# A two-sided third unit in the first phase of a feed-forward layer

## The chip, the cores and the metric

The kernel runs on one core of a Trainium2 chip. The metric is the device time in microseconds (us) of one execution. TensorE (PE) multiplies, VectorE (DVE) and ScalarE (ACT) compute, SyncE (SP) issues the loads; each takes its instructions in the order in which they are written down for it, and they wait for each other through semaphores.

## The reference

The reference is an encoder of two layers on 256 tokens of width 2048, in float32. Each layer adds a mixer (attention and a gated recurrence in the first, pooling and grouped attention in the second) and a feed-forward part. Both layers' feed-forward is touched:

```python
def swiglu(x, w_gate, w_up, w_down):
    return (jax.nn.silu(x @ w_gate) * (x @ w_up)) @ w_down
...
        f = swiglu(x, ffn_w_gate[layer], ffn_w_up[layer], ffn_w_down[layer])
        x = layer_norm(DN_ALPHA * x + f, ln_ffn_g[layer], ln_ffn_b[layer])
```

The hidden width is 5632.

## The kernel before

**Precision.** Every operand is split into a rounded high part and a rest (xTh and xTl for x, yTh and yTl for the hidden columns, whi and wlo for weights). A product takes three matmuls of 128x512: high by low, high by high, low by high (`mm3`, L289 to L292).

**Weights.** A half is 512 KB of weights, two blocks of 128x512. `load_half` has SP load it into one of four buffers named raw (L168); ACT rounds it to whi (L127), DVE subtracts to get wlo (L128). The pairs whi and wlo have their own slots: four in the pool wp, and seven more from the pools that `open_ring` adds. While a half is on PE, a later one is loaded into a free slot, and ACT's whi waits for the slot. A half of a gate or up product lasts 12 matmuls on PE.

**Feed-forward.** The hidden width is cut into 11 units of 512 columns, in three phases (`PHASES`, L69): units 0 to 2, 3 to 6, 7 to 10. A phase computes its units and then multiplies by the matching rows of the down weights, four stretches of 512 output columns, which add up in res.

A unit of phase 0 is whole (`whole`, L507): all of the gate's halves add up in two PSUM banks acc, one for each of the two groups of 128 tokens, then all of up's in two banks mx. The gate passes through silu on ACT into sil, DVE multiplies it by up (L523), and some halves later PE transposes the product (`transpose4`, L274) into a bank that ACT and DVE read as yTh and yTl (L127, L128). The list `later` counts halves down (`half_done`) and then issues what is due; the transposes come 4 and 5 halves after the unit, for the third unit 2 and 3.

A unit of phases 1 and 2 is two-sided (`unit`, L455): gate and up of both groups of tokens go on at once in four banks, c11, c12, c21, c22. The 16 blocks of x are taken as 8 pairs. Five pairs take eight products, as in `whole`. The pairs of `SEVEN` (5, 6, 7) take seven, by a scheme that needs sums of blocks of x (the forms e, f, g, h; L409 to L431) and sums of blocks of weights (z, L445 to L447). Such a pair is loaded in one piece of 1 MB into the single buffer rs (L443); ACT casts it to sh (L444, and L127 for the sums), DVE computes z, sl (L448) and sl of the sums (L128). There is one buffer for rs and one for z, and two each for sh and sl. Four further banks take the products p1, p6, p5 and p7, which enter several of the sums and are added when the unit ends (L484 to L499).

**PSUM.** There are eight banks of 128x512. In phase 0 before the change they are acc (3), tr (2) and mx (3). With `open_banks("sides")` they become two sides, aside and bside, of four each: the four sums of a unit on one side, its p banks and transposes on the other, and the sides change places with each unit. A bank is given out again in turn, and its new user waits for the last reader of the old.

**Order.** The program is written in the order of the loops, and each instruction has a priority, raised by `tc.high_priority` (400 for loads and their casts, 1000 for gate products and some transposes' readers). A scheduler places each engine's instructions by these, and what it placed is the order on the engine.

Of the kernel before, what the change touches and what calls it, by code (L numbers as in the profile page):

```python
# [11 lines left out]
F32 = mybir.dt.float32  # L12
# [6 lines left out]
P = 128  # L19
# [4 lines left out]
NCH = 512  # L24
# [42 lines left out]
HELD = 6  # L67
FREE = 7
PHASES = ((0, 1, 2), (3, 4, 5, 6), (7, 8, 9, 10))  # L69


SEVEN = (5, 6, 7)
PAIRS_FIRST = (0, 1, 2, 3, 5, 4, 6, 7)
PAIRS = (0, 1, 5, 2, 3, 6, 4, 7)
PAIRS_LAST = (0, 1, 5, 2, 6, 3, 4, 7)
# [5 lines left out]
def trunk(ctx: ExitStack, tc: tile.TileContext, a, out):  # L81
# [9 lines left out]
    def open_banks(kind):  # L91

        if banks:
            banks["stack"].close()
        stack = ctx.enter_context(ExitStack())
        pool = stack.enter_context(tc.tile_pool(name="ps", bufs=1, space=PSUM, reuse_waits="tile"))
        banks.update(stack=stack, pool=pool, kind=kind, side=0)
# [22 lines left out]
    def mxp():  # L120
        return bank("mx", 3)
# [26 lines left out]
    first = [True]  # L148
# [33 lines left out]
    later = []  # L182
# [91 lines left out]
    def transpose4(src, hi, lo, ahead_by=0):  # L274
        t = trp()
        for k in range(4):
            transpose(t[:, k * P : (k + 1) * P], src[:, k * P : (k + 1) * P], ident)
        v = t.rearrange("p (k t) -> p k t", k=4)
        with tc.high_priority(offset=ahead_by):
            split(hi, lo, v)  # L280
# [174 lines left out]
    def unit(sp, pairs, sevens, w, lhs, forms, yT, opening):  # L455

        b = {n: side_bank() for n in ("c11", "c21", "c12", "c22")}
        begun = set()
        left = {n: 4 * (len(pairs) - len(sevens)) // 2 for n in b}
        for _, _, n in SEVEN_ORDER:  # L460
            left[n] = left.get(n, 0) + len(sevens)

        def product(name, x, wt):
            left[name] -= 1
            mm3(b[name], x, wt, name not in begun, left[name] == 0)
            begun.add(name)

        behind = [low[-n] if opening and n else None for n in BEHIND]
        for p in pairs:
            if p in sevens:  # L470
                if "p1" not in b:
                    b.update((n, side_bank(True)) for n in ("p1", "p6", "p5", "p7"))
                wt = load_seven(sp, w[p], behind.pop(0))
                for i, x, name in SEVEN_ORDER:
                    product(name, forms[p][x], wt(i))
            else:
                for n, ks in ((0, (2 * p, 2 * p + 1)), (1, (2 * p + 1, 2 * p))):
                    hi, lo = load_half(w[p][:, 2 * n : 2 * n + 2])
                    for tok in range(NT):
                        for kk in range(2):  # L480
                            product(f"c{tok + 1}{n + 1}", lhs(tok, ks[kk]), (hi[:, kk, :], lo[:, kk, :]))
                    half_done()
        with tc.high_priority(offset=1000):
            g0, w_, v, x = (sp.tile([P, NCH], F32, tag=n, name=n, bufs=1) for n in ("g0", "g1", "u0", "u1"))  # L484
            nc.scalar.copy(g0, b["p1"])  # L485
            nc.vector.tensor_tensor(w_, g0, b["p6"], op=sub)
            nc.vector.tensor_tensor(v, w_, b["p5"], op=add)
            nc.vector.tensor_tensor(w_, w_, b["p7"], op=add)
            nc.vector.tensor_tensor(x, w_, b["p5"], op=add)
            nc.vector.tensor_tensor(g0, g0, b["c11"], op=add)  # L490
            nc.scalar.activation(g0, g0, AF.Silu)
            nc.vector.tensor_tensor(v, b["c12"], v, op=sub)
            nc.vector.tensor_tensor(w_, w_, b["c21"], op=add)
            nc.scalar.activation(w_, w_, AF.Silu)
            nc.vector.tensor_tensor(x, b["c22"], x, op=sub)

            banks["side"] ^= 1
            for tok, (g, u) in enumerate(((g0, v), (w_, x))):
                nc.vector.tensor_tensor(g, g, u, op=mult)  # L499
                s = slice(tok * P, (tok + 1) * P)  # L500
                later.append([2 + tok, lambda g=g, s=s: transpose4(g, yT[0][:, :, s], yT[1][:, :, s], 1000)])

    def ffn(layer, xT, res, mix_pool, close_mix, keep, last):
        lhs = x_lhs(xT)
        w = a[f"gu{layer}"]

        def whole(c, pool, first):  # L507

            gouts = [acc() for _ in range(NT)]
            sil = {}  # L510

            def silu(tok):
                sil[tok] = pool.tile([P, NCH], F32, tag="sil", name="sil", bufs=3)
                nc.scalar.activation(sil[tok], gouts[tok], AF.Silu)

            mm_chunk([(w[c, i][:, :2], (2 * i, 2 * i + 1)) for i in range(8)], lhs, gouts, tok_major=first, after=silu)

            uouts = [mxp() for _ in range(NT)]
            y = new_yT()

            def gated(tok):
                with tc.high_priority(offset=1000):
                    nc.vector.tensor_tensor(sil[tok], sil[tok], uouts[tok], op=mult)  # L523
                s = slice(tok * P, (tok + 1) * P)
                later.append([(2 if c == PHASES[0][-1] else 4) + tok, lambda: transpose4(sil[tok], y[0][:, :, s], y[1][:, :, s])])

            mm_chunk([(w[c, i][:, 2:], (2 * i + 1, 2 * i)) for i in range(8)], lhs, uouts, after=gated)
            return y

        stack = ExitStack()  # L530
        forms, making = {}, []

        def make():
            with tc.issue_after(low[-1]):
                if next(making[0], "end") is None:
                    later.append([3, make])

        nxt = cdp = None
        groups = {}
        for pi, chunks in enumerate(PHASES):  # L540
            end = pi == len(PHASES) - 1
            for c in chunks:
                if pi == 0:
                    groups[c] = whole(c, mix_pool, c == 0)
                else:
                    groups[c] = new_yT()
                    pairs = PAIRS_FIRST if c == chunks[0] else PAIRS_LAST if c == chunks[-1] else PAIRS
                    sevens = SEVEN[:-1] if c == chunks[-1] else SEVEN
                    unit(sp, pairs, sevens, w[c], lhs, forms, groups[c], c == chunks[0])
            if pi == 0:  # L550
                close_mix()
                sp = later_pool(stack, f"sp{layer}")
                open_banks("sides")
                making.append(forms_of(sp, xT, forms))
                later.append([2, make])
            gl = [groups[c] for c in chunks]
            if end:
                stack.close()
                open_banks("uses")
                cdp = None if last else keep("cdc")  # L560
                open_ring(keep(f"er{layer}"), 4)
                open_ring(later_pool(stack, f"e{layer}"), 3)
                fp = later_pool(stack, f"g{layer}")
                nxt = None if last else new_xT()
            stats = new_stats()
            evac, norm = residual_tools(res, None, None, None, stats)
            for n in range(4):
                if cdp and n == 1:
                    consts.extend(cd_constants(cdp))
                if end and n == 1:  # L570
                    evac, norm = residual_tools(res, *load_gb(fp, layer, "ffn"), stats)
                outs = [acc() for _ in range(NT)]
                halves = [(a[f"down{layer}"][n, 2 * c + i], two(4 * ci + 2 * i)) for ci, c in enumerate(chunks) for i in range(2)]

                def after(tok):
                    with tc.high_priority(offset=1000 if end and n == 3 else 0):
                        evac(tok, n, outs[tok], pi == 0, end)
                        if end and n == 3:
                            norm(tok, nxt, out if last else None)

                mm_chunk(halves, y_lhs(gl), outs, tok_major=(end and n == 3), after=after)
            if not end:
                banks["side"] ^= 1
        if end:
            rings.pop()
            stack.close()
        return nxt
# [427 lines left out]
    xT = new_xT()  # L1015
# [11 lines left out]
    def later_pool(stack, name):  # L1027
        return stack.enter_context(tc.tile_pool(name=name, bufs=1, reuse_waits="tile"))
# [22 lines left out]
    xT = layer_end(0, a["ab_out"], AB_OUT_GROUPS, yT, False)  # L1051
# [119 lines left out]
```

## Time and profile before

| | us |
|---|---|
| median of 3 runs | 2190.62 (2190.13 to 2190.7) |
| profiled execution | 2193.0 |
| span of the profiled execution, first to last instruction | 2191.2 |
| PE busy | 2172.8 (99%) |
| DVE busy | 1557.9 (71%) |
| ACT busy | 1051.0 (48%) |

The profile is of one execution. The times of its rows count from the first instruction. A timeline row gives the start, the duration, the engine, the line and what is written from what; a bracket gives how long the engine stood idle before it and what ended that. An engine's next instruction can start some 0.08 us ahead of the end that is shown for the last, so what a sequence takes is read from the distance of the starts. A group row gives the number of instructions, their busy time in all and the mean of one in ns, and behind it the engine's idle time ahead of them.

Layer 0's phase 0 ends with the third unit, its up from 624.11 to 645.87 us, and down follows. Layer 1's feed-forward starts at about 1474 us.

### The profile page before, as it was taken

What the parts mean: (1) busy time and instruction counts of PE and PEld (TensorE: products, weight loads), DVE (VectorE), ACT (ScalarE), POOL (GpSimd) and SP (SyncE); (2) the same over time, 40 slices, a digit from 0 to 9 for tenths busy, and PEclk for the clock granted to TensorE, in tenths of its full rate; (3) what the DMA queues carried; (4) which work ended last, traced back from release to release, by engine and by line L of the source; (5) the groups of instructions that cost most, each with busy time, mean ns of one, the idle gap of its engine ahead of it and who ended that gap; (6) DMA issues with size and microseconds to landing.
All of it is one profiled execution on the core that took longest, in us unless ns stands there. A gap on an engine that the chain in (4) does not pass through costs nothing.

```text
span 2191.2 us, 26625 instructions
## 1 busy us (share of the span) xinstructions
PE 2172.8 (99%) x10048; PEld 1803.9 (82%) x10048; DVE 1557.9 (71%) x1954; ACT 1051.0 (48%) x1278; POOL 49.5 (2%) x51
## 2 busy tenths in 40 slices
PE   9999999999999999999999999999999999999997
PEld 7888888888888888888888888888888888888886
DVE  6886688677537788577786775676367896768865
ACT  6445544546425454444445554455344554445441
POOL 0000000000000000000000300000000000000000
PEclk9999999999999999999999999999999999999999
DMA  8555536684636555565548553647456555655473
GB/s 297 162 164 176 170 128 192 200 280 146 232 123 227 185 201 192 187 232 184 194 153 296 174 175 123 229 158 255 143 186 232 183 191 183 220 175 195 173 250 112
DMA packets 112850, 420.64 MB, mean 192 GB/s; under 512 B 13776, under 2 KB 16848, under 8 KB 105808
## 3 DMA queue, kind: packets, MB, share of 16 engines
q1 hardware_dynamic: 112720, 418.93, 57.0%
q8 instruction: 79, 1.29, 0.2%
q14 instruction: 51, 0.42, 0.1%
HBM read 416.78 MB, written 2.10 MB: 191 GB/s over the span
## 4 chain that ended last, share of the span: by engine, by line
PE 94%; DVE 3%; DMA 2%; issue 1%; SPq 0%; ACT 0%; DVEq 0%
PE acc L292 43%; PE bside L292 21%; PE aside L292 19%; PE mx L292 7%; DMA rs<-in_gu 2%; PE mx L729 1%; PE tr L124 1%; DVE wlo L128 1%; DVE sl L128 0%; DVE sl L448 0%; PE mx L775 0%; PE bside L124 0%; PE aside L124 0%; PE mx L988 0%; DMA raw<-in_ab_in 0%
## 5 line engine op out<-in xcount | busy, mean ns | idle before, releaser
L128 DVE TENSOR_TENSOR wlo<-raw,whi 128x1024 fp32r<-128x1024 f32 (+1 forms) x673 | 816.6, 1223 | 433.8 <-ACT whi L127 428.0
L127 ACT CAST whi<-raw 128x1024 fp32r<-128x1024 f32 (+1 forms) x673 | 703.5, 1051 | 815.0 <-PE acc L292 253.8
L292 PE MATMUL acc<-whi,xTl 128*128 128x512 f32 x864 | 343.2, 397 | 4.7 <-ACT whi L127 4.7
L292 PE MATMUL acc<-whi,xTh 128*128 128x512 f32 x864 | 339.8, 393 | 0.0
L292 PE MATMUL acc<-wlo,xTh 128*128 128x512 f32 x864 | 337.5, 393 | 0.1
L292 PE MATMUL acc<-whi,yTl 128*128 128x512 f32 x512 | 200.7, 392 | 0.1
L292 PE MATMUL acc<-whi,yTh 128*128 128x512 f32 x512 | 199.7, 390 | 0.0
L292 PE MATMUL acc<-wlo,yTh 128*128 128x512 f32 x512 | 197.6, 390 | 0.2 <-DVE wlo L128 0.2
L292 PEld LDWEIGHTS acc<-whi,xTl 128*128 128x128 f32 x864 | 162.9, 189 | 36.9 <-ACT whi L127 5.6
L292 PEld LDWEIGHTS acc<-wlo,xTh 128*128 128x128 f32 x864 | 162.7, 188 | 33.9 <-DVE wlo L128 1.1
L292 PEld LDWEIGHTS acc<-whi,xTh 128*128 128x128 f32 x864 | 163.1, 189 | 31.2
L292 PE MATMUL bside<-whi,xTl 128*128 128x512 f32 x336 | 131.9, 393 | 1.5 <-ACT g L485 1.1
L292 PE MATMUL aside<-whi,xTl 128*128 128x512 f32 x336 | 131.2, 391 | 0.2
L292 PE MATMUL bside<-whi,xTh 128*128 128x512 f32 x336 | 131.0, 390 | 0.0
L292 PE MATMUL aside<-whi,xTh 128*128 128x512 f32 x336 | 131.0, 390 | 0.0
L292 PE MATMUL bside<-wlo,xTh 128*128 128x512 f32 x336 | 128.2, 390 | 0.0
L292 PE MATMUL aside<-wlo,xTh 128*128 128x512 f32 x336 | 128.1, 390 | 0.0
L292 PEld LDWEIGHTS acc<-wlo,yTh 128*128 128x128 f32 x512 | 96.2, 188 | 20.6 <-DVE wlo L128 0.7
L292 PEld LDWEIGHTS acc<-whi,yTl 128*128 128x128 f32 x512 | 96.2, 188 | 19.8 <-DVE res L308 0.5
L292 PEld LDWEIGHTS acc<-whi,yTh 128*128 128x128 f32 x512 | 96.2, 188 | 19.3
L128 DVE TENSOR_TENSOR sl<-z,sh 128x2048 fp32r<-128x2048 f32 x44 | 100.7, 2288 | 6.4 <-ACT sh L127 5.7
L444 ACT CAST sh<-rs 128x1536 fp32r<-128x1536 f32 x44 | 65.2, 1482 | 74.6 <-DMA rs<-in_gu 33.7
(266 smaller groups left out, 3445.4 us busy)
## 6 DMA issues: line engine op xcount, KB each, us to landing
raw<-in_gu SPq DMA_DIRECT2D x264, 512.0 KB, 4.7
raw<-in_down SPq DMA_DIRECT2D x176, 512.0 KB, 4.0
raw<-in_ab_in SPq DMA_DIRECT2D x127, 512.0 KB, 4.0
rs<-in_gu SPq DMA_DIRECT2D x44, 1024.0 KB, 6.2
raw<-in_cd_in SPq DMA_DIRECT2D x40, 512.0 KB, 4.3
raw<-in_ab_out SPq DMA_DIRECT2D x32, 512.0 KB, 4.4
raw<-in_cd_out SPq DMA_DIRECT2D x32, 512.0 KB, 4.4
bias<-in_na_bias SPq DMA_DIRECT2D x32, 64.0 KB, 4.2
```

The costliest lines, as they stand in the source:

```text
L124: return nc.tensor.transpose(o, src, eye)
L127: nc.scalar.copy(hi, src)
L128: return nc.vector.tensor_tensor(lo, src, hi.bitcast(F32), op=sub).ins
L292: ins = nc.tensor.matmul(o, lhs[a], rhs[b], start=start and n == 0, stop=stop and n == 2)
L444: nc.scalar.copy(hi[:, :3], raw[:, :3])
L729: nc.tensor.matmul(m[:, 2 * h + s, :], kk[:, h, s * P : (s + 1) * P], qq[:, h, r * P : (r + 1) * P], start=True, stop=True,)
```

## The change

The third unit of phase 0 is computed as a two-sided unit, with `PAIRS` and the three pairs of `SEVEN`. What goes with it:

- The pool that held sil and seven of the slots for whi and wlo is closed, and the pool of the two-sided units (sp) opened, 6 halves into the second unit (`change_rooms`), no longer after the third. sil of the second unit is then in the buffers g0 and g1.
- The forms are made from there on, a step in each half (`make`, once every 3 halves before).
- The banks become sides between the second and the third unit.
- The second unit's transposes come 2 and 3 halves after it, into bside banks, and the two instructions that read each have priority 1000.
- The first unit of phase 1 still orders its pairs by `PAIRS_FIRST`, and its 1 MB loads wait as before.

```diff
@@ -504,13 +505,17 @@
-        def whole(c, pool, first):
+        def whole(c, first):
...
             def silu(tok):
-                sil[tok] = pool.tile([P, NCH], F32, tag="sil", name="sil", bufs=3)
+
+                if sps:
+                    sil[tok] = sps[0].tile([P, NCH], F32, tag=f"g{tok}", name=f"g{tok}", bufs=1)
+                else:
+                    sil[tok] = mix_pool.tile([P, NCH], F32, tag="sil", name="sil", bufs=3)
...
-                later.append([(2 if c == PHASES[0][-1] else 4) + tok, lambda: transpose4(sil[tok], y[0][:, :, s], y[1][:, :, s])])
+                later.append([(4 if first else 2) + tok, lambda: transpose4(sil[tok], y[0][:, :, s], y[1][:, :, s], 0 if first else 1000)])
...
-        forms, making = {}, []
+        forms, making, sps = {}, [], []
 
         def make():
             with tc.issue_after(low[-1]):
                 if next(making[0], "end") is None:
-                    later.append([3, make])
+                    later.append([1, make])
+
+        def change_rooms():
+            close_mix()
+            sps.append(later_pool(stack, f"sp{layer}"))
+            making.append(forms_of(sps[0], xT, forms))
+            later.append([1, make])
...
-                if pi == 0:
-                    groups[c] = whole(c, mix_pool, c == 0)
+                if c < 2:
+                    groups[c] = whole(c, c == 0)
+                    if c == 0:
+                        later.append([6, change_rooms])
+                    else:
+                        open_banks("sides")
                 else:
                     groups[c] = new_yT()
-                    pairs = PAIRS_FIRST if c == chunks[0] else PAIRS_LAST if c == chunks[-1] else PAIRS
-                    sevens = SEVEN[:-1] if c == chunks[-1] else SEVEN
-                    unit(sp, pairs, sevens, w[c], lhs, forms, groups[c], c == chunks[0])
-            if pi == 0:
-                close_mix()
-                sp = later_pool(stack, f"sp{layer}")
-                open_banks("sides")
-                making.append(forms_of(sp, xT, forms))
-                later.append([2, make])
+                    pairs, sevens = PAIRS, SEVEN
+                    if pi and c == chunks[0]:
+                        pairs = PAIRS_FIRST
+                    elif pi and c == chunks[-1]:
+                        pairs, sevens = PAIRS_LAST, SEVEN[:-1]
+                    unit(sps[0], pairs, sevens, w[c], lhs, forms, groups[c], pi and c == chunks[0])
```

DVE before, layer 0, from the products of the second unit (sil by mx) on; the wlo are those of the third unit's halves, tr the banks of the second unit's transposes. The numbers tell buffers apart.

```order
L523 TENSOR_TENSOR sil_5022<-sil_5022,mx_5026 128x512
L523 TENSOR_TENSOR sil_5024<-sil_5024,mx_5027 128x512
L128 TENSOR_TENSOR wlo_5382<-raw_5380,whi_5381 128x1024
L128 TENSOR_TENSOR wlo_5400<-raw_5398,whi_5399 128x1024
L128 TENSOR_TENSOR wlo_5418<-raw_5416,whi_5417 128x1024
L128 TENSOR_TENSOR wlo_5436<-raw_5434,whi_5435 128x1024
L128 TENSOR_TENSOR wlo_5454<-raw_5452,whi_5453 128x1024
L128 TENSOR_TENSOR yTl_5029<-tr_5250,yTh_5028 128x4x128
L128 TENSOR_TENSOR wlo_5472<-raw_5470,whi_5471 128x1024
L128 TENSOR_TENSOR yTl_5029<-tr_5275,yTh_5028 128x4x128
L128 TENSOR_TENSOR wlo_5505<-raw_5503,whi_5504 128x1024
```

Seven instructions after the first product DVE reads the first transposes, and none of them belongs to a 1 MB load.

DVE in the changed kernel, the same place; rs_5398 is the second 1 MB load of the third unit and rs_5467 the third, z and sl belong to them; the lines are one to five higher.

```order
L129 TENSOR_TENSOR wlo_5248<-raw_5246,whi_5247 128x1024
L528 TENSOR_TENSOR g0_5030<-g0_5030,mx_5034 128x512
L528 TENSOR_TENSOR g1_5032<-g1_5032,mx_5035 128x512
L448 TENSOR_TENSOR z_5401<-z_5401,rs_5398 128x512
L129 TENSOR_TENSOR wlo_5273<-raw_5271,whi_5272 128x1024
L129 TENSOR_TENSOR sl_5400<-z_5401,sh_5399 128x2048
L446 TENSOR_TENSOR z_5470<-rs_5467 128x1024
L129 TENSOR_TENSOR wlo_5328<-raw_5326,whi_5327 128x1024
L447 TENSOR_TENSOR z_5470<-z_5470,rs_5467 128x512
L448 TENSOR_TENSOR z_5470<-z_5470,rs_5467 128x512
L129 TENSOR_TENSOR wlo_5346<-raw_5344,whi_5345 128x1024
L129 TENSOR_TENSOR yTl_5037<-bside_5239,yTh_5036 128x4x128
```

The read of the first transposes (bside_5239) now follows the first z of the third load, and the last z of the second load, which sets rs free, stands ahead of both.

PE before, layer 0, at the second unit's first transposes, within the third unit's gate.

```order
L292 MATMUL acc_5177<-whi_5233,xTh1_3821 128x512
L292 MATMUL acc_5177<-wlo_5234,xTh1_3821 128x512
L124 MATMUL tr_5250<-ident_72,sil_5022 128x128 x4
L292 MATMUL acc_5176<-whi_5258,xTl0_3822 128x512
L292 MATMUL acc_5176<-whi_5258,xTh0_3820 128x512
L292 MATMUL acc_5176<-wlo_5259,xTh0_3820 128x512
```

PE goes on in acc, and the bank tr is used again only by the next transposes but one.

PE in the changed kernel, layer 0, at the first pair of seven products; bside_5289 is p1, bside_5290 p6, and bside_5291 is p5, whose bank is that of bside_5239. The transposes into bside_5239 and bside_5264 stand 24 and 12 matmuls ahead of the pair.

```order
L293 MATMUL aside_5202<-wlo_5273,xTh1_3821 128x512
L293 MATMUL bside_5289<-sh_5294,xTl0_3822 128x512
L293 MATMUL bside_5289<-sh_5294,xTh0_3820 128x512
L293 MATMUL bside_5289<-sl_5295,xTh0_3820 128x512
L293 MATMUL bside_5290<-sh_5294,fml_5116 128x512
L293 MATMUL bside_5290<-sh_5294,fmh_5115 128x512
L293 MATMUL bside_5290<-sl_5295,fmh_5115 128x512
L293 MATMUL aside_5199<-sh_5294,xTl0_3822 128x512
L293 MATMUL bside_5291<-sh_5294,fml_5116 128x512
L293 MATMUL bside_5291<-sh_5294,fmh_5115 128x512
L293 MATMUL bside_5291<-sl_5295,fmh_5115 128x512
L293 MATMUL aside_5199<-sh_5294,xTh0_3820 128x512
```

The third product of the pair writes a bank that the transposes had.

On SP the third unit's first 1 MB load stands between the raw loads of the second unit's last two halves, the second behind the raw load of its own second half, the third five raw loads later. In layer 1 the engines' orders are the same.

## Rows read from the trace of the kernel before

**Rows 1.** The page: span, busy time of the engines, and the chain of waits by engine.

```profile
span 2191.2 us, 26625 instructions
...
PE 2172.8 (99%) x10048; PEld 1803.9 (82%) x10048; DVE 1557.9 (71%) x1954; ACT 1051.0 (48%) x1278; POOL 49.5 (2%) x51
...
PE 94%; DVE 3%; DMA 2%; issue 1%; SPq 0%; ACT 0%; DVEq 0%
```

**Rows 2.** What PE waited for: engine, line, what was waited for, us in all, times, the longest.

```profile
PE acc L292 <- ACT whi L127: 4.7, 1, 4.7
PE bside L292 <- ACT g L485: 1.1, 2, 0.8
PE acc L292 <- DVE wlo L128: 0.2, 1, 0.2
```

**Rows 3.** PE's timeline: a block of transposes and the two matmuls behind it, then the first matmul of the third unit's up and the first of down.

```profile
567.79 0.60 PE L124 MATMUL tr<-ident,sil 128*128 128x128 f32 x4
568.14 0.47 PE L292 MATMUL acc<-whi,xTl 128*128 128x512 f32 x1
568.46 0.39 PE L292 MATMUL acc<-whi,xTh 128*128 128x512 f32 x1
...
624.11 0.39 PE L292 MATMUL mx<-whi,xTl 128*128 128x512 f32 x1
...
645.87 0.39 PE L292 MATMUL aside<-whi,yTl 128*128 128x512 f32 x1
```

**Rows 4.** Busy time by window: us, then for each engine busy us and instructions, the granted clock of PE as a share of full, the DMA share and GB/s. The first window holds the second and third unit, the second one down and the beginning of phase 1.

```profile
560.00:645.00 85.00, 85.00 (x385) 70.35 (x384) 35.54 (x34) 30.45 (x33) 0.00 (x0) 1.00 0.50 164
645.00:735.00 90.00, 90.00 (x402) 74.54 (x401) 66.19 (x66) 43.32 (x40) 0.00 (x0) 1.00 0.65 223
```

**Rows 5.** Groups of instructions by line and shape of DVE, and ACT's whi from the page: count, busy us, mean ns, idle time ahead.

```profile
L128 DVE TENSOR_TENSOR wlo<-raw,whi 128x1024 fp32r<-128x1024 f32 x671 | 815.2, 1224 | 432.8 <-ACT whi L127 426.9 <-PE acc L292 1.6 <-DMA raw<-in_ab_in 1.5
L128 DVE TENSOR_TENSOR sl<-z,sh 128x2048 fp32r<-128x2048 f32 x44 | 100.7, 2288 | 6.4 <-ACT sh L127 5.7
L448 DVE TENSOR_TENSOR sl<-rs,sh 128x1536 fp32r<-128x1536 f32 x44 | 77.1, 1753 | 26.6 <-ACT sh L444 26.6
L445 DVE TENSOR_TENSOR z<-rs 128x1024 f32<-128x1024 f32 x44 | 53.7, 1221 | 37.3 <-DMA rs<-in_gu 37.0
L446 DVE TENSOR_TENSOR z<-z,rs 128x512 f32<-128x512 f32 x44 | 30.1, 684 | 0.3
...
L128 DVE TENSOR_TENSOR yTl<-bside,yTh 128x512 fp32r<-128x512 f32 x16 | 10.9, 683 | 2.1 <-ACT yTh L127 2.1
...
L523 DVE TENSOR_TENSOR sil<-sil,mx 128x512 f32<-128x512 f32 x12 | 8.0, 682 | 0.2
```

```profile
L127 ACT CAST whi<-raw 128x1024 fp32r<-128x1024 f32 (+1 forms) x673 | 703.5, 1051 | 815.0 <-PE acc L292 253.8
```

**Rows 6.** Timelines of DVE, SP and ACT at the first 1 MB load of layer 0, in down of phase 0: the last two fs, the load's issue, its first use.

```profile
676.24 0.55 DVE L424 TENSOR_TENSOR fs<-xs 128x384 f32<-128x384 f32 x1
676.71 0.55 DVE L425 TENSOR_TENSOR fs<-xs,fs 128x384 f32<-128x384 f32 x1
```

```profile
677.35 0.33 SPq L443 DMA_DIRECT2D rs<-in_gu  x1
```

```profile
683.59 1.48 ACT L444 CAST sh<-rs 128x1536 fp32r<-128x1536 f32 x1 [0.32 <-DMA rs<-in_gu]
```

**Rows 7.** SP's and ACT's timelines at a 1 MB load of phase 1: a raw load, the 1 MB load, the next raw load, and the first use.

```profile
794.91 0.33 SPq L168 DMA_DIRECT2D raw<-in_gu  x1
797.83 0.33 SPq L443 DMA_DIRECT2D rs<-in_gu  x1
798.91 0.33 SPq L168 DMA_DIRECT2D raw<-in_gu  x1
```

```profile
802.68 1.48 ACT L444 CAST sh<-rs 128x1536 fp32r<-128x1536 f32 x1 [1.14 <-DMA rs<-in_gu]
```

**Rows 8.** The same of SP and DVE at two further 1 MB loads, and from the view of the buffer rs the time from issue to landing of all 44. A raw row with x2 or x4 stands for that many loads.

```profile
811.18 0.33 SPq L168 DMA_DIRECT2D raw<-in_gu  x1
812.98 0.33 SPq L443 DMA_DIRECT2D rs<-in_gu  x1
814.11 8.47 SPq L168 DMA_DIRECT2D raw<-in_gu  x4
...
2017.50 2.06 SPq L168 DMA_DIRECT2D raw<-in_gu  x2
2021.03 0.33 SPq L443 DMA_DIRECT2D rs<-in_gu  x1
```

```profile
819.87 1.23 DVE L445 TENSOR_TENSOR z<-rs 128x1024 f32<-128x1024 f32 x1
...
2028.49 1.23 DVE L445 TENSOR_TENSOR z<-rs 128x1024 f32<-128x1024 f32 x1 [0.67 <-DMA rs<-in_gu]
```

```profile
DMA to landing us min/median/max: 4.6/6.2/8.7
```

**Rows 9.** PE's and ACT's timelines at PE's longest wait after the start, where a unit follows a unit.

```profile
1097.30 0.39 PE L292 MATMUL aside<-sl,xTh 128*128 128x512 f32 x1
1098.50 0.50 PE L292 MATMUL bside<-whi,xTl 128*128 128x512 f32 x1 [0.82 <-ACT g L485]
1098.84 0.40 PE L292 MATMUL bside<-whi,xTh 128*128 128x512 f32 x1
```

```profile
1097.87 0.58 ACT L485 COPY g<-bside 128x512 f32<-128x512 f32 x1
```

**Rows 10.** PE's timeline at the start, and the core's span and mean granted clock.

```profile
4.73 0.80 PE L292 MATMUL acc<-whi,xTl 128*128 128x512 f32 x1 [4.73 <-ACT whi L127]
...
8.04 0.63 PE L292 MATMUL acc<-wlo,xTh 128*128 128x512 f32 x1
8.47 0.63 PE L292 MATMUL acc<-whi,xTl 128*128 128x512 f32 x1
8.90 0.44 PE L292 MATMUL acc<-whi,xTh 128*128 128x512 f32 x1
```

```profile
core 0: 2191.2 us, clock 0.998
```

## The prediction

> **What bounds the kernel now.** I read the page's busy line and chain of waits first, then the waits of PE, then PE's timeline, and last the lines of DVE and the timelines around the 1 MB loads. PE is busy 2172.8 of 2191.2 us, and 94% of the chain of waits is PE [rows 1]. After the start PE waits only 1.3 us by name: 1.1 us for the copy that opens a unit's end (ACT L485) and 0.2 us for one wlo [rows 2]. So a matmul less is a matmul's time less, and any wait that is put in front of PE is paid in full. In the third unit of layer 0 (gate from 601.5 us, up 624.11 to 645.87) 96 matmuls lie between the first rows of up and of down: (645.87 − 624.11) / 96 = 0.2267 us each. Four transposes in between cost PE about 0.35 + 0.32 − 0.2267 = 0.44 us [rows 3]. In that stretch PE is busy 85.00 of 85.00 us while DVE works 35.54 [rows 4]: DVE has room, but it takes its instructions in the order written.
>
> **What the change removes.** Three pairs of the third unit take seven products in place of eight, three matmuls each: 9 matmuls fewer a layer, 18 in all, 18 × 0.2267 = 4.08 us. Bytes loaded are the same, the raw loads only grow from 0.5 to 1 MB for those pairs.
>
> **What it moves at no cost.** The forms (xs, fs, fmh, fml) are made in the second unit's up instead of in down; the same instructions, on a DVE that has 49 of 85 us free there [rows 4]. The rings shrink from eleven whi and wlo to four, halfway through the second unit's gate. A half lasts PE 12 × 0.2267 = 2.72 us and DVE needs 1.14 us from start to start for its wlo; the later phases run on four already, and PE is busy 90.00 of 90 us there [rows 4]. If that cover were gone, each late half would show as a PE wait on wlo, of which there is 0.2 us now [rows 2]. The end of the third unit becomes that of a two-sided unit, ten DVE instructions in place of two, but down opens with the first unit's columns, and needs the third's four halves later.
>
> **What it adds: a wait behind a load.** The second unit's transposes go into two of the four bside banks. The first pair of seven products takes the other two for p1 and p6, and for p5 and p7 it must take the transposes' banks again, so PE stops before p5 until DVE has read the first of them (yTl). In before they had tr banks for which nobody waited. In the changed DVE queue that read stands behind the first z of the third 1 MB load, and DVE can't pass it. So the load's landing decides. The priority given to the reads does not lift yTl above that z.
>
> Set U = 0 at the third unit's first matmul. PE asks for the bank after 48 matmuls of two pairs, 7 of p1, p6 and c11, and two blocks of transposes: 55 × 0.2267 + 2 × 0.44 = 13.35.
>
> DVE's side, start to start as the timelines show it (0.08 under each duration): wlo 1.14, z 1.14 then 0.60 twice, sl 1.67 and 2.21, a gate's product 0.60, yTl 0.60 and 0.68 to its end [rows 5]; ACT's whi 1.05.
> - First load. Its buffer is that of xs, so it goes out after the last two fs. They stand behind the wlo whose whi slot comes free 108 matmuls before U: −24.5, whi to −23.45, wlo to −22.2, two fs of 0.47 to −21.2. The same sequence in before: fs at 676.24 and 676.71, issue 677.35, landed just before 683.59, 6.2 us [rows 6]. With 6.3 it is there at −14.9.
> - z 1.14, wlo 1.14, z 0.60, sl 1.67, z 0.68 free the buffer: the second load goes out at −9.6. The nearest row has a raw load 2.9 us ahead and another 1.1 behind: 797.83 to 802.68, 4.85 us at most [rows 7]. It lands at −4.8, while DVE still has wlo, wlo, sl 2.21 and wlo, 5.63 in all, until −4.0.
> - From −4.0: z 1.14, sl 1.67, wlo 1.14, z 0.60, wlo 1.14, two gate products 1.20, z 0.68: the third load goes out at +3.6.
> - The third load goes out 1.8 and 3.5 us behind two raw loads, and a third follows 1.1 later. Two loads in before stand exactly so: issued 812.98, used 819.87 (6.9 us); issued 2021.03, used 2028.49 with DVE waiting for it (7.5) [rows 8]. I take 7.2: +10.8. The group of all 44 gives 4.6 at least and 8.7 at most [rows 8].
> - Behind it z 1.14, wlo 1.14, z 0.60, z 0.60, wlo 1.14 and the read 0.68, with its release 5.4: +16.2.
> PE waits 16.2 − 13.35 = 2.85 us, and a restart costs 0.11 more (1098.50 to 1098.84 is 0.34 against 0.2267) [rows 9]: 2.96 a layer, 5.92 in two. The second read follows 1.7 us later, and PE needs its bank 2.5 us after the first, so p7 adds nothing.
>
> Before, no bank is awaited here, so the wait's price is bounded by the loads: third at 4.85 gives 13.85, a stall of 0.5 and with the restart 0.6; third at 8.7 gives 4.35; and if the second load took 7.4 too, 1.6 more, 5.95. The lower end is below that: with every load early DVE reads in time and the price is 0; a gain has no reason, since nothing here was awaited. I take 2.96, since two rows have the third load's very neighbours.
>
> On the load, the Trainium skill has another price (SBUF — State Buffer, "The DMA setup-cost knee"): about 2 us fixed and the bytes at 436 GB/s, an estimate of 4.4 us for 1 MB. By that the read would end near 13.4, and the sum would be the removed matmuls alone. The least of the 44 loads, 4.6, agrees with the skill's figure; the two beside raw loads, 6.9 and 7.5, do not, and this load has three beside it.
>
> Sum on the profiled execution: 2193.0 − 4.08 + 5.92 = 2194.8 us. It lies 2.4 us over the runs' median of 2190.62; the same difference, +1.84, on the median gives **2192.5 us**.
>
> **The rivals.** About 0.2% (4.4 us) is the least a measurement of this kernel can tell from no change: 2186.24 to 2195.0.
> - No stall worth naming, because the loads land alone (4.85 us) or DVE comes there early. For it: the least of the 44 loads is 4.6, one among traffic took 4.85, and DVE is idle for over half of this stretch. Against it: the two rows with these very neighbours. Time: 2190.62 − 4.08 + 2 × 0 to 0.6 = 2186.5 to 2187.7. Chance 0.15.
> - The slower side: the second load also meets traffic. Then third issue and read move by 1.6 us, and with 7.2 to 8.7 for the third the stall is 4.45 to 5.95, 5.3 with the restart on the mean, in each layer: 2190.62 − 4.08 + 10.6 = 2197.1. It decides from a stall of (4.38 + 4.08) / 2 = 4.2 us a layer. For it: the median of the 44 loads is 6.2, the most 8.7 [rows 8]. Against it: the one row with the second load's neighbours [rows 7]. Chance 0.15.
> - PE comes back from the stall at half pace. At the start ten matmuls from 4.73 to 8.90 stand some 0.43 us apart (8.04 to 8.47), the pace of the 1.2 GHz level, and from there at half of that; the run's mean granted clock is 0.998 [rows 10] and that of the stretch here 1.00 [rows 4]. 4.17 us so would cost 4.17 × (1 − 0.2267 / 0.427) = 1.95 a layer, 3.9 in all: 2196.4. Against it: the longest wait in before, 1.2 us, was followed by a spacing of 0.34 and no slow stretch [rows 9]; a wait of 3 us isn't in the trace. Chance 0.06. The Trainium skill tells of this rule (TensorE: Matmul & The Clock Gate, "HAM oscillation — how this bites in real kernels"): a PE that waits for data between groups falls back to the half clock. The wait of 1.2 us does not show it, and no row here has a longer one.
> - The end of the third unit holds down up: its p1 is copied by ACT behind a load's cast, as after 1097.30, where PE lost 1.20 − 0.23 + 0.11 = 1.1 us [rows 9]. Twice that on top of the forecast: 2194.7. Against it: p1 is complete 18 matmuls, 4.1 us, before down opens, and a cast and the copy take ACT 1.05 + 0.58. Chance 0.04.
>
> **How the numbers follow.** The forecast, a stall of 1 to 4.2 us a layer, has 0.60 and by itself 2188.5 to 2195.0. Faster: only the best of the first rival, 0.05. Same: the forecast, the rest of that rival and the last one, 0.74. Slower: the second and third, 0.21. The range goes from the first rival's time to the second's: 2186.4 to 2197.2.
>
> **What would show it.** In the profile after: PE's waits must list a bside matmul of L293 waiting for yTl (DVE L129), twice, 2 to 4 us each, at the first pair of seven products. DVE's waits must show z waiting for rs just before, and PE's matmul count must fall by 18. If PE's waits do not change, the first rival holds and the time falls by 4. A load that takes under 5 us or over 8 there, a slow spacing behind the wait, or PE waiting elsewhere (for whi, for g L486) would make the forecast wrong.

## The result and the profile after

| | us |
|---|---|
| changed kernel, median of 5 runs | 2199.43 (2197.53 to 2203.79) |
| kernel before, median of 5 runs | 2190.62 (2190.13 to 2191.64) |
| ratio, after to before | 1.0043, 95% interval 1.0032 to 1.0054 |
| forecast | 2192.5, range 2186.4 to 2197.2, no change that can be told |

The change makes the kernel slower: by 0.43% in the ratio, by 8.8 us between the medians. The time lies above the range. The page after, as [rows 1], and the core's clock, as [rows 10]:

```profile
span 2197.7 us, 26597 instructions
...
PE 2171.8 (99%) x10030; PEld 1802.9 (82%) x10030; DVE 1589.2 (72%) x1988; ACT 1059.2 (48%) x1280; POOL 49.9 (2%) x51
...
PE 92%; DVE 4%; DMA 2%; issue 1%; SPq 0%; ACT 0%; DVEq 0%
```

```profile
core 0: 2197.7 us, clock 0.996
```

PE issues 10030 matmuls where it issued 10048: the 18 are gone. Yet its busy time fell by 1.0 us and not by 4, which says that some of the others took longer. The clock, 0.998 before, says the same. What PE waited for, as [rows 2]:

```profile
PE bside L293 <- DVE yTl L129: 8.7, 2, 4.4
PE acc L293 <- ACT whi L128: 4.7, 1, 4.7
PE acc L293 <- DVE wlo L129: 0.2, 1, 0.2
```

The first row is new: a bside matmul waits for yTl, twice, 4.4 us at most. PE's timeline shows the place in layer 0 (p1, p6, one matmul of c11, then p5) and what follows:

```profile
601.50 0.39 PE L293 MATMUL aside<-whi,xTl 128*128 128x512 f32 x1
...
614.48 0.39 PE L293 MATMUL bside<-sl,fmh 128*128 128x512 f32 x1
614.71 0.39 PE L293 MATMUL aside<-sh,xTl 128*128 128x512 f32 x1
619.48 0.79 PE L293 MATMUL bside<-sh,fml 128*128 128x512 f32 x1 [4.39 <-DVE yTl L129]
620.08 0.63 PE L293 MATMUL bside<-sh,fmh 128*128 128x512 f32 x1
620.50 0.63 PE L293 MATMUL bside<-sl,fmh 128*128 128x512 f32 x1
...
623.49 0.60 PE L293 MATMUL aside<-sh,xTh 128*128 128x512 f32 x1
623.92 0.41 PE L293 MATMUL aside<-sl,xTh 128*128 128x512 f32 x1
624.16 0.39 PE L293 MATMUL bside<-sh,fml 128*128 128x512 f32 x1
```

Two losses stand here. From 614.71 to 619.48 are 4.77 us, 4.54 more than a matmul. From 619.48 to 623.92 ten matmuls begin in 4.44 us, 2.17 more than 10 × 0.2267: they stand 0.43 us apart, as at the start [rows 10]. The granted clock by window (the columns are those of [rows 4]) names the cause:

```profile
614.94:619.48 4.54, 0.15 (x1) 0.00 (x0) 4.50 (x7) 1.04 (x1) 0.00 (x0) 0.74 0.33 112
619.48:623.92 4.44, 4.44 (x11) 3.47 (x12) 2.81 (x3) 0.00 (x0) 0.00 (x0) 0.50 0.77 236
623.92:630.00 6.08, 6.08 (x28) 5.04 (x27) 3.61 (x2) 4.24 (x3) 0.00 (x0) 1.00 0.38 119
```

Over the wait the mean is 0.74, so the clock fell while PE stood still. Right behind the wait it is at 0.50, the 1.2 GHz level, and then at 1.00. The wait ends with DVE's read of the first transposes, and DVE's timeline tells what that stood behind:

```profile
607.96 2.29 DVE L129 TENSOR_TENSOR sl<-z,sh 128x2048 fp32r<-128x2048 f32 x1 [0.85 <-ACT sh L128]
614.00 1.23 DVE L446 TENSOR_TENSOR z<-rs 128x1024 f32<-128x1024 f32 x1 [3.75 <-DMA rs<-in_gu]
615.14 1.22 DVE L129 TENSOR_TENSOR wlo<-raw,whi 128x1024 fp32r<-128x1024 f32 x1
616.28 0.69 DVE L447 TENSOR_TENSOR z<-z,rs 128x512 f32<-128x512 f32 x1
617.00 0.69 DVE L448 TENSOR_TENSOR z<-z,rs 128x512 f32<-128x512 f32 x1
617.61 1.22 DVE L129 TENSOR_TENSOR wlo<-raw,whi 128x1024 fp32r<-128x1024 f32 x1
618.74 0.68 DVE L129 TENSOR_TENSOR yTl<-bside,yTh 128x512 fp32r<-128x512 f32 x1
```

DVE stands idle for 3.75 us in front of z, which waits for the third load, and the read comes sixth in the queue, counted from that z. ACT's half of the same read was done long before:

```profile
609.73 0.57 ACT L128 CAST yTh<-bside 128x512 fp32r<-128x512 f32 x1
```

Layer 1 repeats it: 1568.48 to 1573.22, then seven matmuls in 3.10 us.

```profile
1568.48 0.39 PE L293 MATMUL aside<-sh,xTl 128*128 128x512 f32 x1
1573.22 0.79 PE L293 MATMUL bside<-sh,fml 128*128 128x512 f32 x1 [4.34 <-DVE yTl L129]
...
1575.94 0.54 PE L293 MATMUL aside<-sh,fmh 128*128 128x512 f32 x1
1576.32 0.40 PE L293 MATMUL aside<-sl,fmh 128*128 128x512 f32 x1
```

That is 4.51 for the wait and 3.10 − 7 × 0.2267 = 1.51 for the slow matmuls. The sum is −4.08 + 4.54 + 4.51 + 2.17 + 1.51 = +8.65 us, against 8.81 between the medians. Between the two profiled spans it is only 6.5 us (2191.2 to 2197.7), since the profiled execution of the kernel before lies 2.4 us above its median; its trace has waits of PE for g, 1.1 us in all [rows 2], that the trace after does not have.

### The profile page after: what moved, and what is told of

The parts are those of the page before. It is cut to its first block, busy times and chain, and to the rows that moved or that the text cites. A ratio compares the mean times of both kernels' runs of the same rounds, so it can differ in the third digit from the quotient of the medians.

```text
span 2197.7 us, 26597 instructions
## 1 busy us (share of the span) xinstructions
PE 2171.8 (99%) x10030; PEld 1802.9 (82%) x10030; DVE 1589.2 (72%) x1988; ACT 1059.2 (48%) x1280; POOL 49.9 (2%) x51
## 4 chain that ended last, share of the span: by engine, by line
PE 92%; DVE 4%; DMA 2%; issue 1%; SPq 0%; ACT 0%; DVEq 0%
PE acc L293 40%; PE aside L293 23%; PE bside L293 20%; PE mx L293 4%; DMA rs<-in_gu 2%; PE mx L741 1%; PE tr L125 1%; DVE wlo L129 1%; DVE sl L129 1%; DVE sl L449 0%; PE mx L787 0%; PE bside L125 0%; PE aside L125 0%; PE mx L1000 0%; DMA raw<-in_ab_in 0%
## 5 line engine op out<-in xcount | busy, mean ns | idle before, releaser
L129 DVE TENSOR_TENSOR wlo<-raw,whi 128x1024 fp32r<-128x1024 f32 (+1 forms) x661 | 801.1, 1223 | 368.8 <-ACT whi L128 362.6
L128 ACT CAST whi<-raw 128x1024 fp32r<-128x1024 f32 (+1 forms) x661 | 690.6, 1051 | 757.6 <-PE acc L293 257.4
L293 PE MATMUL acc<-whi,xTl 128*128 128x512 f32 x800 | 317.9, 397 | 4.8 <-ACT whi L128 4.7
L293 PE MATMUL acc<-whi,xTh 128*128 128x512 f32 x800 | 315.0, 394 | 0.0
L293 PE MATMUL acc<-wlo,xTh 128*128 128x512 f32 x800 | 312.4, 393 | 0.0
L293 PE MATMUL aside<-whi,xTl 128*128 128x512 f32 x416 | 162.6, 391 | 0.1
L293 PE MATMUL aside<-whi,xTh 128*128 128x512 f32 x416 | 162.1, 390 | 0.0
L293 PE MATMUL aside<-wlo,xTh 128*128 128x512 f32 x416 | 159.0, 390 | 0.0
L129 DVE TENSOR_TENSOR sl<-z,sh 128x2048 fp32r<-128x2048 f32 x50 | 114.5, 2289 | 10.0 <-ACT sh L128 9.2
L128 ACT CAST sh<-z 128x2048 fp32r<-128x2048 f32 x50 | 95.7, 1913 | 34.0 <-DVE z L448 33.7
```

What stands on the lines that cost most here:

```text
L128: nc.scalar.copy(hi, src)
L129: return nc.vector.tensor_tensor(lo, src, hi.bitcast(F32), op=sub).ins
L293: ins = nc.tensor.matmul(o, lhs[a], rhs[b], start=start and n == 0, stop=stop and n == 2)
```

## The experiments

The theory (Q in the expectations): all of the loss is the read in DVE's queue behind the third load, with the slow pace behind the wait. The rivals: the moved work costs something too (M); the banks are too few in any order (B); and, on the slow pace, that it follows any wait or any long one (H), or no wait, so that a wait costs its length alone (L). Each variant was run beside the kernel before, which took 2188.7 to 2189.1 us there.

**DVE's order: z_behind_reads.** The third load still goes out where it did; its sums are issued after the second read. The orders of ACT and SP are those of the changed kernel. PE's differs by one place in each layer: p5 directly follows p6, where one matmul of c11 stood between them, so PE asks for the bank one matmul earlier in the order.

```diff
+            if read:
+                order.enter_context(tc.issue_after(read))
             nc.vector.tensor_tensor(z[:, :2], raw[:, 0:3:2], ...
...
-                wt = load_seven(sp, w[p], behind.pop(0))
+                wt = load_seven(sp, w[p], behind.pop(0), reads[-1] if third and p == 7 else None)
```

Expected:

> Only DVE's order differs from the changed kernel: the third 1 MB load's sums (z, sl) stand behind the two reads of the second unit's transposes; the load goes out as before. Theory Q (the whole loss is that read standing in DVE's queue behind a load, and the slow pace of PE after it): PE's waits for yTl go, so does the stretch of 0.43 us spacing, and what is left is 18 matmuls less: 2190.6 - 4.1 = 2186.5 us, 2185 to 2187.5. Theory M (shrinking the rings, making the forms early and the new end of the unit cost something too): the wait goes, but the time stays above 2188. Theory B (four bside banks are too few at this place, whatever DVE does first): PE still waits for yTl, 2 us or more a layer, about 2191 to 2195.

Measured: ratio 0.9981 (0.9972 to 0.9990), 2184.33 against 2188.9 us. 0.0019 of 2188.9 is 4.2 us (the interval is 2.2 to 6.1), where the 18 matmuls are 4.08 us. PE's waits hold no yTl, and the read stands ahead of z:

```profile
612.46 0.68 DVE L129 TENSOR_TENSOR yTl<-bside,yTh 128x512 fp32r<-128x512 f32 x1
613.06 1.22 DVE L129 TENSOR_TENSOR wlo<-raw,whi 128x1024 fp32r<-128x1024 f32 x1
614.19 0.68 DVE L129 TENSOR_TENSOR yTl<-bside,yTh 128x512 fp32r<-128x512 f32 x1
614.79 1.22 DVE L449 TENSOR_TENSOR z<-rs 128x1024 f32<-128x1024 f32 x1
```

```profile
615.03 0.39 PE L294 MATMUL bside<-sh,fml 128*128 128x512 f32 x1
```

The read ends at 613.1, 1.9 us before p5 (615.03 here), although the load took 7.75 us to land, against 7.91 in the changed kernel. So M and B fall: rings, forms and the new end of the unit cost nothing that can be measured (by the interval, less than 2 us), and four bside banks are enough with this order. This version is faster than both kernels.

**The sums behind two casts only: z_behind_casts.** As before, with the sums behind the wlo of pair 2's second half in place of the reads.

```diff
-                wt = load_seven(sp, w[p], behind.pop(0))
+                wt = load_seven(sp, w[p], behind.pop(0), low[-5] if third and p == 7 else None)
```

Expected:

> The third load's first z stands behind two more wlo, but still directly ahead of the first read. With the load used at 614.00 as in the changed kernel, the read ends at 614.00 + 1.14 + 0.68 = 615.8, and PE asks at 614.94. Theory Q: a wait of 0.9 us a layer (0.3 to 1.8), and with the shorter wait no slow stretch: 2190.6 - 4.1 + 2 x 1.0 = 2188.6. Theory H (any wait here is followed by the slow stretch of some 2 us): 2190.6 - 4.1 + 2 x (1.0 + 1.8) = 2192.1. Theory B: the wait stays at 4.5 us, since the same instructions stand ahead of the read.

Measured: 0.9984 (0.9975 to 0.9993), and no wait for yTl at all.

```profile
613.00 1.22 DVE L448 TENSOR_TENSOR z<-rs 128x1024 f32<-128x1024 f32 x1 [0.55 <-DMA rs<-in_gu]
614.14 0.68 DVE L129 TENSOR_TENSOR yTl<-bside,yTh 128x512 fp32r<-128x512 f32 x1
```

```profile
615.49 0.39 PE L293 MATMUL bside<-sh,fml 128*128 128x512 f32 x1
```

The forecast wait of 0.9 us was missed for two reasons that the rows show: the load was there at 613.0, a microsecond sooner than in the changed kernel, and PE, whose order moved too, asks two matmuls later in it, at 615.49. B falls again. On the slow pace the run says nothing, since there was no wait.

**PE asks later: pairs_first.** `PAIRS_FIRST` for the third unit; DVE's order at the place stays.

```diff
-                    pairs, sevens = PAIRS, SEVEN
+                    pairs, sevens = PAIRS if pi else PAIRS_FIRST, SEVEN
```

Expected:

> The third unit's order of pairs is (0, 1, 2, 3, 5, 4, 6, 7): PE asks for the banks of p5 and p7 some 48 matmuls later, 10.9 us, and the read is done by then. DVE's order at the place is the same. Theory B (banks): no wait left, 2186.5. Theory Q: the queue behind the load holds the wlo of the fifth half too; it ends at 615.14 + 1.22 = 616.36, and PE wants it as the third matmul of that half, 601.6 + 48 x 0.2267 + 0.88 + 0.45 = 613.8: a wait of PE for wlo of about 2.5 us a layer in place of the one for yTl, 2190.6 - 4.1 + 2 x 2.6 = 2191.7, up to 2195.5 with a slow stretch behind it.

Measured: 1.0003 (0.9994 to 1.0013). PE waits for another result of the same queue, the wlo of the fifth half, for 2.0 us and 1.9 us from matmul to matmul:

```profile
PE aside L293 <- DVE wlo L129: 3.2, 2, 1.6
```

```profile
613.70 0.39 PE L293 MATMUL aside<-whi,xTh 128*128 128x512 f32 x1
615.74 0.50 PE L293 MATMUL aside<-wlo,xTh 128*128 128x512 f32 x1 [1.65 <-DVE wlo L129]
616.07 0.39 PE L293 MATMUL aside<-whi,xTl 128*128 128x512 f32 x1
616.30 0.40 PE L293 MATMUL aside<-whi,xTh 128*128 128x512 f32 x1
```

So it is DVE's queue that is held up by the load, and the bank is only the first to feel it. The wait is about 0.5 us shorter than theory Q had it, since the third load was used at 613.32 here. Behind these shorter waits the spacing is 0.33 once and then 0.23: no slow pace in the profiled execution. It is one of ten; in three of the others the core's mean clock is 0.997, which none of the 33 executions of the kernel before shows (0.998 and 0.999), so there PE may have slowed down behind the wait.

**Without the third load: two_sevens.** Pair 7 of the third unit takes eight products.

```diff
-                    pairs, sevens = PAIRS, SEVEN
+                    pairs, sevens = PAIRS, SEVEN if pi else SEVEN[:-1]
```

Expected:

> The third unit takes seven products for the pairs 5 and 6 alone, pair 7 takes eight: no third 1 MB load in the unit, and 12 matmuls fewer than before in all. Everything else of the change is there. Theory Q: no wait for yTl, 2190.6 - 12 x 0.2267 = 2187.9. Theory M: above 2189. Theory B: still a wait for yTl of 2 us or more.

Measured: 0.9990 (0.9981 to 0.9999), 2.2 us faster, where 12 matmuls are 2.7. PE's waits hold no yTl. As theory Q has it. A 1 MB load still goes out at this place (605.52), now the next unit's, but both reads stand ahead of its sums on DVE (611.95 and 613.68). So a load at this place does not hold PE by itself.

**Is the precedence a part of it: no_precedence.** The priority of the two reads at 0. No engine's order differs from the changed kernel's, so the run is the changed kernel once more.

```diff
-... transpose4(sil[tok], y[0][:, :, s], y[1][:, :, s], 0 if first else 1000)])
+... transpose4(sil[tok], y[0][:, :, s], y[1][:, :, s])])
```

Expected:

> The changed kernel with the priority of the second unit's reads back at 0. The order on all engines is the same as in the changed kernel, so theory Q says the same wait for yTl, twice, about 4.5 us, and 1.004 of the kernel before: the precedence is no part of the loss and none of a gain. A rival, that the precedence brought the reads forward, would have the wait longer by the instructions passed, 1 us or more a layer, 1.005 or more.

Measured: 1.0039 (1.0024 to 1.0054), as theory Q has it, with waits of 3.99 and 3.75 us from matmul to matmul. The third load took less here, z starts at 613.37 in place of 614.00, and the wait is shorter by about as much. The slow pace is there again in both layers:

```profile
619.90:623.00 3.10, 3.10 (x9) 2.38 (x8) 1.75 (x3) 0.00 (x0) 0.00 (x0) 0.50 0.88 287
...
1570.00:1575.30 5.30, 5.30 (x13) 4.14 (x14) 2.79 (x3) 0.00 (x0) 0.00 (x0) 0.50 0.74 244
```

In layer 0 the first three matmuls behind the wait still stand 0.23 to 0.34 apart (618.84, 619.18, 619.41, 619.65), the next 0.29, and only then 0.43; in layer 1 thirteen matmuls take 5.63 us from 1569.99, 2.68 more than at full pace. The clock can fall a little after the wait, and how long it stays low differs.

**A wait without a load: long_read_4 and long_read_6.** On top of z_behind_reads the first read is repeated four and six more times; the repetitions write the same values.

```diff
+            for _ in range(again):
+                nc.vector.tensor_tensor(lo, v, hi.bitcast(F32), op=sub)
```

Expected:

> The kernel with the third load's sums behind the reads, and the first read of the second unit's transposes repeated four more times with the same result, so that the bank is set free later without any load deciding it: by the times of the run z_behind_reads the fourth repetition ends at 618.4, 3.5 us after PE asks (614.94). Theory L (a wait of this length costs its length alone): 2 x 3.5 more than that run, 0.9981 + 7.0 / 2190 = 1.0013 of the kernel before, and spacing 0.23 us from the second matmul on. Theory H (PE falls to the slow pace behind a wait that is long enough, and 3.5 us is): some 2 us a layer more, 1.003, with a stretch of 0.43 us spacing behind each wait; the waits of 2.0 and 1.9 us in pairs_first had none, those of 4.5 us in the changed kernel had 2.2 and 1.5 us of loss.

> As long_read_4, with six repetitions: the last ends at 622.0, a wait of 7.0 us a layer. Theory L: 0.9981 + 14 / 2190 = 1.0045. Theory H with a slow stretch of a length of its own: as after 4.5 us, 1.5 to 2.2 us a layer more, 1.0061. If the slow stretch grows with the wait: 3 us a layer or more, above 1.007.

Measured: 0.9987 (0.9978 to 0.9996) and 0.9984 (0.9975 to 0.9994). Both expectations failed: there is no wait for yTl. The repetitions are on DVE where they were expected (the fourth ends at 618.23 + 0.68 = 618.91), but PE's order changed with them: eight further matmuls of the pair and seven of the next half now stand ahead of p5, which starts at 618.63 in the same trace.

```profile
618.23 0.68 DVE L284 TENSOR_TENSOR yTl<-bside,yTh 128x512 fp32r<-128x512 f32 x1
```

```profile
618.41 0.39 PE L296 MATMUL aside<-whi,xTl 128*128 128x512 f32 x1
618.63 0.39 PE L296 MATMUL bside<-sh,fml 128*128 128x512 f32 x1
```

p5 starts ahead of that repetition's end because in these two kernels it has the bank of the second transposes, whose read ends at 617.2, and p7, which comes later still, that of the first. So the scheduler that writes the orders put other products in front of the longer DVE work; in the changed kernel, with its wait behind the load, it had left p5 where it was. That it can count DVE work and not a load's time would explain this; no run shows it. On H and L the two runs say nothing.

**Other products first: p5_last.** To get a wait between 2 and 3.5 us, p5 and p7 come last in the pair.

```diff
+                order = sorted(SEVEN_ORDER, key=lambda e: e[2] in ("p5", "p7")) if third and p == sevens[0] else SEVEN_ORDER
-                for i, x, name in SEVEN_ORDER:
+                for i, x, name in order:
```

Expected:

> In the third unit's first pair of seven products p5 and p7 are computed last. The order on DVE, ACT and SP stays that of the changed kernel at this place, with the read of the transposes behind the third load; PE does the 15 matmuls of p1, p6, c11, c12, c21 and c22's shares first and asks for p5's bank 8 matmuls later, 1.8 us. Theory Q: the read ends when it did, so the wait shrinks by 1.8 us, from 3.5 to 4.6 (changed kernel and no_precedence) to 1.7 to 2.8 us a layer. If waits under 3 us leave PE at full pace, as those of 2.0 and 1.9 us did: 2 x 2.3 - 4.1 = +0.5 us, ratio 1.000. If such a wait has the slow stretch behind it already: 2 x (2.3 + 1.9) - 4.1 = +4.3 us, 1.002. Theory B (too few banks whatever the order): the wait stays at 3.5 us or more, 1.004.

Measured: 1.0018 (1.0008 to 1.0028).

```profile
616.84 0.39 PE L293 MATMUL aside<-sl,xTh 128*128 128x512 f32 x1
619.58 0.50 PE L293 MATMUL bside<-sh,fml 128*128 128x512 f32 x1 [2.35 <-DVE yTl L129]
619.92 0.40 PE L293 MATMUL bside<-sh,fmh 128*128 128x512 f32 x1
620.16 0.40 PE L293 MATMUL bside<-sl,fmh 128*128 128x512 f32 x1
621.31 0.50 PE L293 MATMUL bside<-sh,fml 128*128 128x512 f32 x1 [0.76 <-DVE yTl L129]
```

```profile
621.70:625.00 3.30, 3.30 (x10) 2.58 (x9) 2.10 (x2) 2.91 (x2) 0.00 (x0) 0.53 0.84 223
```

The first wait of layer 0 shrinks to 2.51 us (2.74 from matmul to matmul), as expected, and B falls there a third time. What was not expected: p7 now waits for the second read (0.92 us), since it follows p5 at once, and the clock falls behind the two waits together. In layer 1 the second load took longer and the wait is 3.76 us (1566.73 to 1570.72), so that layer tells nothing on B. The second load, which landed after 4.7 to 5.2 us in both layers of the changed kernel and of the other variants that keep the read at its place, took 6.7 here. The slow pace is not in every execution of this kernel: of nine, six have a mean clock of 0.996 or 0.997, three have the 0.998 or 0.999 of the kernel before.

## Why the prediction was wrong

The mechanism and its place were right: the moved work costs nothing that can be measured, 18 matmuls are 4.08 us, PE stops before p5 in both layers for yTl, and DVE waits there for the third load. PE asks 614.71 + 0.23 − 601.50 = 13.44 us after U, where 13.35 was worked out. Two terms failed: the length of the stall, and the slow pace behind it, which the sum had left out.

- **The loads' durations.** SP's timeline has the three loads, as [rows 6 to 8]:

```profile
580.33 0.33 SPq L444 DMA_DIRECT2D rs<-in_gu  x1
...
592.94 0.33 SPq L444 DMA_DIRECT2D rs<-in_gu  x1
...
606.00 0.33 SPq L444 DMA_DIRECT2D rs<-in_gu  x1
```

  The first goes out at U − 21.2, exactly as forecast, and is used by DVE at 587.64, 7.3 us later, where 6.3 was taken from a single row. So the second goes out at U − 8.6 in place of −9.6, and the third at U + 4.5 in place of +3.6; that one is used 8.0 us later in place of 7.2. 0.9 and 0.8 make the 2.85 us stall one of 4.5. All loads together keep the spread of [rows 8]: 4.7 at least, 9.0 at most. The step that failed is the choice of one value in the middle for three loads in a row, where a late load moves the next one. The rows could have warned of it: beside the two loads of [rows 8] the trace before has two more with the third load's neighbours, used 6.9 and 8.05 us after their issue. The slower of them, with DVE waiting for it:

```profile
1070.97 0.33 SPq L443 DMA_DIRECT2D rs<-in_gu  x1
1079.02 1.23 DVE L445 TENSOR_TENSOR z<-rs 128x1024 f32<-128x1024 f32 x1 [1.27 <-DMA rs<-in_gu]
```

  The first load's row had the right neighbours too (1.0 us behind one raw load, 1.7 ahead of the next, in both kernels), and yet the load took longer here. Why stays open. The price of the slower side has a slip as well: by its own times a second load of 7.4 us moves what follows by 1.8 us, not 1.6.
- **The slow pace.** "PE comes back from the stall at half pace" was a rival of its own with a chance of 0.06, so the sum has it at nothing. Its price, 1.95 us a layer, was about right: 2.17 and 1.51. It is no rival but follows from the stall when that is long. In the profiled executions, from matmul to matmul, gaps of 1.20 us [rows 9] and of 1.89 and 2.04 (pairs_first) left the clock at 1.00; all five of 3.75 to 4.77 us, in three kernels, were followed by a clock of 0.50. The forecast stall of 2.85 us, a gap of 3.08, lay between them, and in p5_last gaps of 2.74 and 1.15, with three matmuls between them, together had the slow pace. The other executions agree: the mean clock is 0.996 or 0.997 in all nine of the changed kernel and of no_precedence, and 0.998 or 0.999 in all 64 of the kernel before that were run beside the variants. The Trainium skill's rule (TensorE: Matmul & The Clock Gate, "HAM oscillation — how this bites in real kernels"), that a PE that waits for data falls back to the half clock, agrees with these rows; the prediction set it aside for a row with a wait too short to tell.

The slower side was right in kind: a stall over 4.2 us a layer, 2197.1. With the slow pace on top, 3.7 us as measured, it would have been 2200.8, 1.4 us over the measured 2199.43. The rivals were priced apart, and their sum was no case. The first rival's time, that of no stall, is what z_behind_reads gave (0.9981 of before), but by another order on DVE and not by early loads. The last rival, the end of the unit, is not seen: no PE wait for g L486 in the trace after.

The Trainium skill's price of a 1 MB load (SBUF — State Buffer, "The DMA setup-cost knee"), an estimate of 4.4 us, comes near the least load of the trace after too, 4.7 us, and not the first and third loads here.

## What to carry to other kernels

Where an engine takes its instructions in order, a result that another engine waits for must not stand behind an instruction that waits for a load; look in the order for the first such instruction ahead of it, not at how busy the engine is. A priority does not help if it changes no order: compare the order with and without it. Price a stall of PE together with the slow pace behind it, and price a chain of loads by the late end of the rows too, since a late load delays the next: here 0.9 and 0.8 us added up.

## What the runs showed of the hardware that was not expected

In a kernel in which PE is otherwise busy 99% of the time, its granted clock fell to 0.50 in or right behind each single wait of 3.5 to 4.5 us that was profiled. Where the cost was counted it was 1.5 to 2.7 us beside the wait (2.17, 1.51, 1.73 and 2.68 us). Two waits of 2.51 and 0.92 us close together did the same. In the third units of the changed kernel and its variants the 1 MB load that goes out 1.8 us behind a 0.5 MB load took 6.8 to 8.0 us to land, the one that goes out 2.9 us behind one 4.7 to 5.2 us, with one of 6.7. In two_sevens the load at the first of these places, the next unit's, took 6.05 and 8.36 us. What sets the time within these ranges is not shown.
